# Prompt attention scores as three half-height products per head, two heads side by side, in place of two full-height products

## The chip, the cores and the metric

The kernel runs on one core of a Trainium2 chip. The metric is the device time of one execution in microseconds; the median of the runs of the kernel before is 925.88 us (three runs, 924.18 to 926.4).

## What is computed

One step of a streaming encoder layer: 512 prompt rows and 32 sample rows of 1024 features, all in float32. A projection gives queries, keys, values and gates for two attention mixers. Mixer A has 16 query heads on 4 key heads and a window of three chunks; mixer B has 16 heads with keys of their own and reaches over all earlier chunks. Both end in a gated sum, an output projection and a convolutional feed-forward part. Cut to what matters here:

```python
def attend(q, k, v, bias, sink):
    s = jnp.einsum('bqngd,bknd->bngqk', q, k, preferred_element_type=jnp.float32) * (HEAD_DIM ** -0.5) + bias
    if sink is not None:
        col = jnp.broadcast_to(sink.astype(jnp.float32)[:, :, None, None], s.shape[:-1] + (1,))
        p = jax.nn.softmax(jnp.concatenate([s, col], axis=-1), axis=-1)[..., :-1]
    else:
        p = jax.nn.softmax(s, axis=-1)
    return jnp.einsum('bngqk,bknd->bqngd', p.astype(v.dtype), v)
```

The head dimension is 64, half of the 128 rows of TensorE.

## The kernel before

All activations lie feature by row and token by column. Every float32 operand of a product is kept as two parts, a high part h in the type float32r and the rest l = x - h, so that a product of x and w is h·w_h + l·w_h + h·w_l (`triple`, line 220). TensorE (PE) does nearly all of the work in such triples: the projections run weight tile by weight tile over the 544 columns in two halves of 272 (`dense`, line 232), eight row blocks of 128 each.

Attention is laid between these triples. `Stream` (line 69) keeps a modelled clock of PE; after every triple `step` may run a piece of attention whose modelled latency is over, or start the next head when its queries, keys and values are due and the pace `PACE_A` or `PACE_B` has run out. The resulting program is then put in order for each engine by a scheduler with a timeline of its own, so neighbours in the text need not be neighbours in PE's queue.

Each pair of heads has 128 feature rows, head 0 in rows 0 to 63 and head 1 in rows 64 to 127. Before the scores, `load_q` (line 439) makes one stack of 128 rows for each head: the high part in the head's own 64 rows (ScalarE, line 445) and the low part in the other 64 (VectorE, line 446). The keys are doubled to match: `kh` has the high part twice, above and below, and `kl` the low part twice. The own half is written by `split` (lines 430 and 431), the other half by a DMA from SBUF to SBUF (`dup`, line 434). So a tile of 128 queries needs two products of full height (line 499): stack times `kh` gives qh·kh + ql·kh, and stack times `kl` adds qh·kl + ql·kl. In mixer B every one of the 8 pairs has keys of its own (`pair_b`, line 765, four key tiles and four such DMAs a pair); in mixer A four query heads share a key head (`group_a`, line 691, and `load_ka`, line 639).

`attend_prompt` (line 528) does one head: four tiles of queries, each with two products into a PSUM bank of the pool `psa` (five banks) and a VectorE instruction that adds the bias and takes the row maximum (line 501). In mixer A each tile has 256 key columns; in mixer B the four tiles have 256, 256, 384 and 512. Then come the softmax (ScalarE line 485, GpSimd line 493), the transposes of the probabilities, their split into `pt_h` and `pt_l`, the products with `v` and `fold`. The sample rows have their own small products; those of `pts` with `v_s` (lines 741 and 855) fill only 64 of PE's columns, for the two heads of a pair in the two halves of the columns.

```python
        for t, (pc, k0, n, bc) in enumerate(geo):
            qs = q[:, 128 * t:128 * t + 128]
            scores(p[:, pc:pc + n], [qs, qs], [x[:, k0:k0 + max(n, 256)] for x in (kh, kl)], bias[:, bc:bc + n],
                   floor, mx[:, t:t + 1])
```

Of the kernel before, what the change touches and what calls it, by code (L numbers as in the profile page):

```python
# [8 lines left out]
F32 = mybir.dt.float32  # L9
F32R = mybir.dt.float32r  # L10
# [5 lines left out]
NP = 512  # L16
# [42 lines left out]
PACE_A, PACE_B, PACE_S = 7.09, 5.87, 1.44  # L59
# [9 lines left out]
class Stream:  # L69
# [74 lines left out]
def body(ctx, tc, a, o):  # L144
# [349 lines left out]

    def scores(out, lhs, rhs, bias, floor, mx):
# [4 lines left out]
        ps = ps[:, :out.shape[1]]  # L500
        V.tensor_tensor_reduce(out=out, in0=ps, in1=bias, op0=ALU.add, op1=ALU.max, scale=1.0,  # L501
                               scalar=floor, accum_out=mx)
# [19 lines left out]
    def fetch(name, i, cols, src):  # L522
        t = ap.tile([128, cols], F32, name=name)
        v = t[:, :src.shape[1]]
        load(v, src, "bias")
        return v

    def attend_prompt(q, kh, kl, bias, floor, sinkcol, geo, groups, vt, hh, dst, dh, scored, done):


        p = ap.tile([128, 1280], F32, name="p")
        mx = ap.tile([128, 4], F32, name="mx", bufs=4)
        tiles = []
        for t, (pc, k0, n, bc) in enumerate(geo):
            qs = q[:, 128 * t:128 * t + 128]
            scores(p[:, pc:pc + n], [qs, qs], [x[:, k0:k0 + max(n, 256)] for x in (kh, kl)], bias[:, bc:bc + n],
                   floor, mx[:, t:t + 1])
            tiles.append(slice(pc, pc + n))
        scored()
        with tc.high_priority(LATER):  # L540
            softmax(p, tiles, mx, sinkcol)
        yield LAT_SOFT
        pts = []
        for blocks, n, _ in groups:
            pts.append(transposed(p, blocks, n))
        yield LAT_PT
        po = bank(psa)
        started = False
        last = groups[-1][2][-1]
        for (h, l), (_, _, prods) in zip(pts, groups):  # L550
            for pr in prods:
                j, c, oc, w = pr
                for x in (h, l):
                    mm(po[:, oc:oc + w], lhsT=vt[:, j, hh, :, :], rhs=x[:, c:c + w],
                       start=not started, stop=pr is last and x is l, skip_group_check=True)
                    started = True
        fold(po, dst[:, :NP], dh, NP)
        done()
# [132 lines left out]
    def group_a(j, ka, va):  # L691
# [11 lines left out]
        kuse = Join(4, lambda _: pe.release("k", 2))  # L703
        vuse = Join(4, lambda _: pe.release("v", 1))

        def scored():
            pe.release("q", 1)
            kuse.one()
# [8 lines left out]
        for u in range(2):  # L717
            pe.reserve("q", 2, 5)
            st2 = [ap.tile([128, NP], F32R, name="q", bufs=5) for _ in range(2)]
            ready = []  # L720
            qready.append(ready)

            def sample(zn, u=u):
                for hh, own, other in pair_rows():
                    h = 2 * u + hh
                    nc.scalar.copy(qsam[own, h], zn[own])
                    V.tensor_tensor(qsam[other, h], zn[own], rr(qsam)[own, h], ALU.subtract)
            for hh in range(2):
                h = 4 * j + 2 * u + hh

                def start(bias, u=u, hh=hh, st2=st2, h=h):
                    sc = col("sink", h)
                    return attend_prompt(st2[hh], kh, kl, bias, sc, sc, a_geo, a_groups, vt, half,
                                         oa[u], hh, scored, finished)
                pe.queue(lambda h=h: fetch("bias", h, 512, a["alibi"][h]), start, (ready, ka[2], va[2]), PACE_A)
            dense(head_norm(0, load_q(st2, sample, ready)))

        def pv(po, pt):
            for hh, own, _ in pair_rows():
                for b in range(2):  # L740
# [5 lines left out]
        pe.queue(lambda: fetch("bias_s", j, 288, a["alibi_s"][j]),  # L746
                 lambda bias: attend_sample([q, q], [ka[3][half], ka[4][half]], bias, sc, sc, 2, A_BLK, pv,
# [17 lines left out]
    def pair_b(i, ob, one):  # L765
# [3 lines left out]
        st2 = [ap.tile([128, NP], F32R, name="q", bufs=5) for _ in range(2)]  # L769
# [6 lines left out]
        dense(head_norm(1, load_q(st2, sample, qr)))  # L776
# [10 lines left out]
        def write(s, c0, cn, zn):  # L787
            n = min(cn, NP - c0)
            if s == 0:
                split(ks_hi[:, NS:], ks_lo[:, NS:], raw, G)  # L790
            for hh, own, _ in pair_rows():
                split(kh[hh][own, c0:c0 + n], kl[hh][own, c0:c0 + n], zn[own, :n])
            nc.sync.dma_start(out=o["kb"][i, :, c0:c0 + cn], in_=zn)
            if s == 1:
                split(ks_hi[:, :NS], ks_lo[:, :NS], zn[:, NP - c0:])
                for hh, own, other in pair_rows():
                    dup(kh[hh], own, other)
                    dup(kl[hh], own, other)
                kr.append(pe.clock + LAT_NORM + LAT_DMA)
# [7 lines left out]
        def scored():  # L807
            pe.release("q", 1)
            pe.release("k", 2)
# [4 lines left out]
        for hh in range(2):  # L814
# [7 lines left out]
    def group_b(g):  # L822
# [35 lines left out]
        for u in range(2):  # L858
# [3 lines left out]
        pe.queue(lambda: fetch("bias_s", g, 288, a["rel_s"][g]),  # L862
                 lambda bias: attend_sample(lhs, rhs, bias, -3.0e38, None, 3, B_BLK, pv,
                                            obs, scored_s, finished_s),
                 pairs[1][3], PACE_S, 2)
# [366 lines left out]
```

## Time and profile before

| | |
|---|---|
| median of the runs | 925.88 us |
| the profiled execution, its own time | 924.88 us |
| span of the profiled execution | 923.0 us |
| PE busy | 898.6 us (97%) |
| VectorE (DVE) busy | 723.6 us (78%) |
| ScalarE (ACT) busy | 542.2 us (59%) |
| GpSimd (POOL) busy | 379.1 us (41%) |
| mean granted clock of PE | 0.994 |
| score products of the prompt (line 85, `ps<-k,q`) | 256, from 54.0 to 468 us |

The profile shows one execution. A PE product is listed from its start to a modelled end, so neighbours overlap; what a product costs is read from the distance between starts. "PEld" is the load of a product's stationary operand, which can run ahead of the product. A row of a timeline that ends in xN merges N like instructions: its start is that of the first, its length reaches to the end of the last.

### The profile page before, as it was taken

Reading aid. Unit: us, or ns where it says so; the run is one execution under the profiler, and the core shown is the slowest. Engines: PE = TensorE matmul, PEld = TensorE weight load, DVE = VectorE, ACT = ScalarE, POOL = GpSimd, SP = SyncE. Lnnn points to the kernel's source line nnn. Section 1 sums busy time; section 2 is a strip of 40 time slices with the busy share of each in tenths; the row PEclk is TensorE's granted clock in tenths of the full one; section 3 lists DMA queues with packets and bytes.
Section 4 is the critical chain, followed back from the end, with each engine's and each line's share of the span. In section 5 each row is a group of like instructions: output and inputs, shape, how many; then the busy total and the mean of one; then the engine's idle time right before and its main releaser. Section 6 shows DMA issues by size and latency. Waiting matters only on the chain.

```text
span 923.0 us, 18908 instructions
## 1 busy us (share of the span) xinstructions
PE 898.6 (97%) x7085; PEld 884.4 (96%) x7085; DVE 723.6 (78%) x1471; ACT 542.2 (59%) x1285; POOL 379.1 (41%) x578
## 2 busy tenths in 40 slices
PE   8879999999999999999999999999999999999998
PEld 7879899989989999999999999999999999999998
DVE  7799876868888888998866558768777776886996
ACT  5568777778878777777764244344444443534542
POOL 6534457465876777766541103221222221100100
PEclk9999999999999999999999999999999999999999
DMA  6222222322334443434415222222222222332342
GB/s 216 83 82 88 71 90 85 101 81 75 109 118 122 135 124 109 129 110 136 133 59 168 89 92 92 92 77 85 92 93 92 84 87 83 96 101 81 119 145 67
DMA packets 40012, 94.38 MB, mean 102 GB/s; under 512 B 4944, under 2 KB 16240, under 8 KB 39920
## 3 DMA queue, kind: packets, MB, share of 16 engines
q1 hardware_dynamic: 39920, 93.17, 31.8%
q8 instruction: 56, 0.92, 0.4%
q14 instruction: 36, 0.29, 0.1%
HBM read 80.48 MB, written 7.10 MB: 95 GB/s over the span
## 4 chain that ended last, share of the span: by engine, by line
PE 76%; DVE 9%; ACT 4%; POOL 3%; issue 2%; DMA 0%; DVEq 0%; POOLq 0%
PE ps L85 73%; PE ps L89 3%; ACT p L485 2%; DVE q L446 1%; DVE zn L422 1%; DVE p L501 1%; DVE w_lo L204 1%; POOL p L493 1%; DVE s L254 1%; DVE t_b L319 1%; DVE k L431 1%; POOL t_sql L414 1%; POOL z L421 1%; DVE pt_l L512 0%; DMA k<-k 0%
## 5 line engine op out<-in xcount | busy, mean ns | idle before, releaser
L85 PE MATMUL ps<-xh,w_lo 128*128 128x272 f32 x1536 | 446.3, 292 | 5.1 <-DVE w_lo L204 5.1
L85 PE MATMUL ps<-xh,w_hi 128*128 128x272 f32 x1536 | 446.0, 292 | 2.7 <-ACT z L412 1.7
L85 PE MATMUL ps<-xl,w_hi 128*128 128x272 f32 x1536 | 446.3, 291 | 0.8 <-DVE xl L327 0.8
L85 PEld LDWEIGHTS ps<-xh,w_lo 128*128 128x128 f32 x1536 | 291.6, 190 | 6.5 <-DVE w_lo L204 6.0
L85 PEld LDWEIGHTS ps<-xh,w_hi 128*128 128x128 f32 x1536 | 291.5, 190 | 4.8 <-ACT z L412 1.9
L85 PEld LDWEIGHTS ps<-xl,w_hi 128*128 128x128 f32 x1536 | 292.0, 190 | 2.1 <-DVE xl L327 1.7
L204 DVE TENSOR_TENSOR w_lo<-w_raw,w_hi 128x1024 fp32r<-128x1024 f32 (+2 forms) x112 | 143.2, 1279 | 30.8 <-ACT w_hi L203 18.3
L201 POOL TENSOR_SCALAR w_hi<-w_raw 128x1024 fp32r<-128x1024 f32 (+2 forms) x62 | 66.6, 1075 | 90.2 <-PE ps L85 70.3
L493 POOL TENSOR_SCALAR p<-p,rc 128x256 f32<-128x256 f32 (+3 forms) x128 | 74.2, 596 | 41.4 <-DVE rc L491 38.0
L203 ACT CAST w_hi<-w_raw 128x1024 fp32r<-128x1024 f32 x50 | 52.6, 1051 | 64.9 <-issue 36.1
L85 PE MATMUL ps<-s,w_hi 128*128 128x272 f32 x448 | 84.0, 288 | 0.0
L485 ACT ACTIVATE p<-p,nm 128x256 f32<-128x256 f32 (+3 forms) x128 | 65.4, 514 | 27.8 <-DVE nm L482 27.7
L938 POOL TENSOR_SCALAR state_u<-u 128x2 f32<-128x2 f32 x44 | 17.1, 388 | 148.7 <-DVE u L935 148.7
L85 PE MATMUL ps<-s 128*128 128x272 f32 (+1 forms) x483 | 71.3, 293 | 1.7 <-DVE s L372 1.7
L85 PEld LDWEIGHTS ps<-s,w_hi 128*128 128x128 f32 x448 | 70.1, 188 | 0.0
L935 DVE TENSOR_TENSOR u<-ps,rstd 128x272 f32<-128x272 f32 x88 | 38.5, 441 | 39.6 <-PE ps L85 37.0
L85 PEld LDWEIGHTS ps<-s 128*128 128x128 f32 x483 | 65.1, 190 | 2.2 <-DVE s L372 1.7
L85 PE MATMUL ps<-s,w_lo 128*128 128x272 f32 x224 | 63.8, 288 | 0.0
L85 PE MATMUL ps<-k,q 128*128 128x256 f32 (+2 forms) x256 | 52.1, 308 | 3.5 <-DMA k<-k 1.8
L414 POOL TENSOR_TENSOR t_sql<-t_sq,t_sqh 128x272 fp32r<-128x272 f32 x52 | 52.7, 1014 | 3.7
L421 POOL TENSOR_TENSOR z<-z,t_y 128x272 f32<-128x272 f32 x52 | 42.7, 822 | 23.9 <-ACT t_y L316 21.7
L512 DVE TENSOR_TENSOR pt_l<-ps,pt_h 128x512 fp32r<-128x512 f32 (+1 forms) x80 | 45.6, 602 | 5.5 <-ACT pt_h L511 4.4
(166 smaller groups left out, 1635.1 us busy)
## 6 DMA issues: line engine op xcount, KB each, us to landing
w_raw<-in_w_in SPq DMA_DIRECT2D x50, 512.0 KB, 3.4
w_raw<-in_w_up SPq DMA_DIRECT2D x44, 512.0 KB, 3.3
w_raw<-in_w_pair SPq DMA_DIRECT2D x16, 512.0 KB, 3.4
k<-k SPq DMA_DIRECT2D x40, 128.0 KB, 2.3
bias<-in_rel SPq DMA_DIRECT2D x16, 256.0 KB, 2.7
w_raw<-in_w_out SPq DMA_DIRECT2D x8, 512.0 KB, 3.5
s<-in_x SPq DMA_DIRECT2D x15, 272.0 KB, 5.7
w_raw<-in_w_down SPq DMA_DIRECT2D x6, 512.0 KB, 3.3
```

The costliest lines, as they stand in the source:

```text
L85: return self.nc.tensor.matmul(out, lhsT=lhsT, rhs=rhs, **kw)
L89: return self.nc.tensor.transpose(out, src, ident)
L201: G.tensor_scalar(hi[:, c], raw[:, c], 1.0, 1.0, ALU.mult, ALU.mult)
L203: nc.scalar.copy(hi[:, c], raw[:, c])
L204: V.tensor_tensor(lo[:, c], raw[:, c], rr(hi)[:, c], ALU.subtract)
L414: G.tensor_tensor(sql, sq, rr(sqh), ALU.subtract)
L421: G.tensor_tensor(z, z, y, ALU.mult)
L485: act(p[:, sl], p[:, sl], AF.Exp, bias=nm[:, t:t + 1], accum_out=sm[:, t:t + 1])
L493: G.tensor_scalar(p[:, sl], p[:, sl], rc[:, t:t + 1], 1.0, ALU.mult, ALU.mult)
L512: V.tensor_tensor(l[:, :n], ps[:, :n], rr(h)[:, :n], ALU.subtract)
L935: V.tensor_tensor(u[:, 2 + c0:2 + c0 + cn], ps, rstd2[:, c0:c0 + cn], ALU.mult)
L938: G.tensor_scalar(state_u[:, m, 0:2], u[:, NP:NP + 2], 1.0, 1.0, ALU.mult, ALU.mult)
```

## The change

Two heads are scored at once. `load_q` keeps the pair's queries as they lie, in one tile of high parts and one of low parts; there are no stacks. For each tile of queries two banks are taken, and each head gets three products of 64 rows: qh·kh, qh·kl and ql·kh (the product ql·kl is left out). Head 0's products use rows 0 to 63 of PE, head 1's rows 64 to 127, and the program text alternates between the two. In mixer B the keys need not be doubled: the 32 DMAs of `dup` go, and a pair has two key tiles in place of four. Mixer A's keys stay doubled, since a key head meets queries of both halves. The softmax and the value part stay one per head (`values`, with a later start for the second head), the bias of two heads is fetched into one tile, and the modelled clock counts a product of 64 rows as half.

```diff
-PACE_A, PACE_B, PACE_S = 7.09, 5.87, 1.44
+LAT_TWO = 4.5
+PACE_A, PACE_B, PACE_S = 12.6, 10.2, 1.44
...
-        self.clock += max(n / 2350, 0.108)
+
+        self.clock += max(n / 2350, 0.108) * (0.5 if lhsT.shape[0] == 64 else 1)
...
-    def load_q(stacks, sample, ready):
-
+    def load_q(qh, ql, sample, ready):
         def write(s, c0, cn, zn):
             n = min(cn, NP - c0)
-            for hh, own, other in pair_rows():
-                q = stacks[hh]
-                nc.scalar.copy(q[own, c0:c0 + n], zn[own, :n])
-                V.tensor_tensor(q[other, c0:c0 + n], zn[own, :n], rr(q)[own, c0:c0 + n], ALU.subtract)
+            split(qh[:, c0:c0 + n], ql[:, c0:c0 + n], zn[:, :n])
...
+        ps = [ap.tile([128, 1280], F32, name="p", bufs=4) for _ in range(2)]
+        mx = [ap.tile([128, 4], F32, name="mx", bufs=6) for _ in range(2)]
         tiles = []
         for t, (pc, k0, n, bc) in enumerate(geo):
-            qs = q[:, 128 * t:128 * t + 128]
-            scores(p[:, pc:pc + n], [qs, qs], [x[:, k0:k0 + max(n, 256)] for x in (kh, kl)], bias[:, bc:bc + n],
-                   floor, mx[:, t:t + 1])
+            banks = [bank(psa) for _ in range(2)]
+            w = max(n, 256)
+            for i, (x, y) in enumerate(((0, 0), (0, 1), (1, 0))):
+                for hh, own, _ in pair_rows():
+                    mm(banks[hh][:, :w], lhsT=q[x][own, 128 * t:128 * t + 128], rhs=ks[hh][y][own, k0:k0 + w],
+                       start=i == 0, stop=i == 2)
+            for hh in range(2):
+                biased(ps[hh][:, pc:pc + n], banks[hh], bias[:, hh, bc:bc + n], floor[hh], mx[hh][:, t:t + 1])
             tiles.append(slice(pc, pc + n))
         scored()
-        with tc.high_priority(LATER):
-            softmax(p, tiles, mx, sinkcol)
-        yield LAT_SOFT
+        for hh in range(2):
+            with tc.high_priority(LATER):
+                softmax(ps[hh], tiles, mx[hh], sinkcol and sinkcol[hh])
+            pe.run(values(ps[hh], groups, vt, vh[hh], dst, hh, done))
+        return
+        yield
+
+    def values(p, groups, vt, vh, dst, hh, done):
+        yield LAT_SOFT + LAT_TWO * hh
...
-        pe.reserve("k", 4, 8)
+        pe.reserve("k", 2, 8)
         pe.reserve("ks", 1, 2)
-        kh = [ap.tile([128, NP], F32R, name="k", bufs=8) for _ in range(2)]
-        kl = [ap.tile([128, NP], F32R, name="k", bufs=8) for _ in range(2)]
+        kh, kl = (ap.tile([128, NP], F32R, name="k", bufs=8) for _ in range(2))
...
-            for hh, own, _ in pair_rows():
-                split(kh[hh][own, c0:c0 + n], kl[hh][own, c0:c0 + n], zn[own, :n])
+            split(kh[:, c0:c0 + n], kl[:, c0:c0 + n], zn[:, :n])
             nc.sync.dma_start(out=o["kb"][i, :, c0:c0 + cn], in_=zn)
             if s == 1:
                 split(ks_hi[:, :NS], ks_lo[:, :NS], zn[:, NP - c0:])
-                for hh, own, other in pair_rows():
-                    dup(kh[hh], own, other)
-                    dup(kl[hh], own, other)
-                kr.append(pe.clock + LAT_NORM + LAT_DMA)
+                kr.append(pe.clock + LAT_NORM)
...
-        for hh in range(2):
-            def start(bias, hh=hh):
-                return attend_prompt(st2[hh], kh[hh], kl[hh], bias, -3.0e38, None, b_geo, b_groups, vt, hh,
-                                     ob, hh, scored, finished)
-            pe.queue(lambda hh=hh: fetch("bias", i, 512, a["rel"][2 * i + hh]), start, (qr, kr, vr), PACE_B)
+
+        def start(bias):
+            return attend_prompt(qn, [(kh, kl)] * 2, bias, [-3.0e38] * 2, None, b_geo, b_groups, vt, (0, 1),
+                                 ob, scored, finished)
+        pe.queue(lambda: fetch("bias", 512, a["rel"][2 * i], a["rel"][2 * i + 1]), start, (qr, kr, vr), PACE_B)
```

PE's queue at the first scores of mixer A, before. A row is a product: the bank it writes, then the moving and the stationary operand, then the size of the result. `ps_744` to `ps_756` are the banks of head 0's four query tiles, `q_230` its stack, `k_207` and `k_209` the doubled keys, and `ps_788` belongs to a projection:

```order
L85 MATMUL ps_788<-xh0_109,w_lo_457 128x272
L85 MATMUL ps_744<-k_207,q_230 128x256
L85 MATMUL ps_744<-k_209,q_230 128x256
L85 MATMUL ps_748<-k_207,q_230 128x256
L85 MATMUL ps_748<-k_209,q_230 128x256
L85 MATMUL ps_788<-xh1_123,w_hi_456 128x272
```

The same place in the changed program, and, fifteen projection products further on, the rest of the second tile and part of the third. `q_230` and `q_231` are the pair's high and low queries; `ps_740` and `ps_741` are the banks of head 0 and of head 1 for the first tile, `ps_750` that of head 0 for the second, `ps_751` that of head 1 for the second, and `ps_760` that of head 0 for the third:

```order
L87 MATMUL ps_720<-xh6_160,w_hi_458 128x272
L87 MATMUL ps_740<-k_207,q_230 128x256
L87 MATMUL ps_741<-k_207,q_230 128x256
L87 MATMUL ps_740<-k_209,q_230 128x256
L87 MATMUL ps_741<-k_209,q_230 128x256
L87 MATMUL ps_750<-k_207,q_230 128x256
L87 MATMUL ps_750<-k_209,q_230 128x256
L87 MATMUL ps_720<-xl6_161,w_hi_458 128x272
L87 MATMUL ps_720<-xh6_160,w_lo_459 128x272
L87 MATMUL ps_740<-k_207,q_231 128x256
L87 MATMUL ps_741<-k_207,q_231 128x256
L87 MATMUL ps_750<-k_207,q_231 128x256
```

```order
L87 MATMUL ps_824<-xh3_142,w_lo_459 128x272
L87 MATMUL ps_751<-k_207,q_230 128x256
L87 MATMUL ps_751<-k_209,q_230 128x256
L87 MATMUL ps_751<-k_207,q_231 128x256
L87 MATMUL ps_824<-xh4_150,w_hi_458 128x272
L87 MATMUL ps_760<-k_207,q_230 128x256
L87 MATMUL ps_760<-k_209,q_230 128x256
L87 MATMUL ps_760<-k_207,q_231 128x256
L87 MATMUL ps_824<-xl4_151,w_hi_458 128x272
```

The text's alternation stands in the first tile; from the second on the scheduler has put the three products of one head together, and products of a projection between the heads. Over the whole queue the 384 products of 64 rows stand in 77 unbroken runs (48 of three products, 17 of six, 5 of nine, 4 of twelve, 3 of fifteen); 47 of the runs hold one head alone. Of the 307 neighbours within runs 118 are of different heads.

VectorE's queue where the first pair's queries are written, before and after (`zn` is the normed pair, 272 and 240 columns of it):

```order
L446 TENSOR_TENSOR q_230<-zn_563,q_230 64x272
L446 TENSOR_TENSOR q_231<-zn_563,q_231 64x272
L204 TENSOR_TENSOR w_lo_643<-w_raw_641,w_hi_642 128x1024
L446 TENSOR_TENSOR q_230<-zn_582,q_230 64x240
L446 TENSOR_TENSOR q_231<-zn_582,q_231 64x240
```

```order
L321 SCALAR_TENSOR_TENSOR t_b_579<-ps_573,eps_80,t_b_579 128x272
L463 TENSOR_TENSOR v_217<-ps_626,v_217 128x8x64
L424 SCALAR_TENSOR_TENSOR zn_582<-t_b_579,z_443 128x272
L292 TENSOR_TENSOR s_636<-ps_687,rstd_179 128x272
L433 TENSOR_TENSOR q_231<-zn_565,q_230 128x272
L433 TENSOR_TENSOR q_231<-zn_582,q_230 128x240
```

Two instructions on all 128 rows stand where four on 64 rows stood; ScalarE's copies halve in the same way, and so do those of mixer B's keys.

## Rows read from the trace of the kernel before

**Rows 1.** The page: busy time, share of the span and instructions of each engine.
```profile
PE 898.6 (97%) x7085; PEld 884.4 (96%) x7085; DVE 723.6 (78%) x1471; ACT 542.2 (59%) x1285; POOL 379.1 (41%) x578
```

**Rows 2.** The page: the chain that ended last, share of the span by engine.
```profile
PE 76%; DVE 9%; ACT 4%; POOL 3%; issue 2%; DMA 0%; DVEq 0%; POOLq 0%
```

**Rows 3.** Busy us of each engine in the stretch of the scores.
```profile
core 0: us, PE busy (x) PEld busy (x) DVE busy (x) ACT busy (x) POOL busy (x), PEclk, DMA share, GB/s
54.00:468.00 414.00, 400.62 (x3175) 390.60 (x3174) 344.70 (x800) 317.27 (x891) 256.40 (x335) 0.99 0.34 104
```

**Rows 4.** Timeline: the eight score products of mixer B's last head, the product behind.
```profile
466.54 1.45 PE L85 MATMUL ps<-k,q 128*128 128x256 f32 x8
...
467.83 0.29 PE L85 MATMUL ps<-xh,w_hi 128*128 128x272 f32 x1
```

**Rows 5.** Timeline: 64-column products, then four scores of mixer A, then a triple.
```profile
114.64 0.46 PE L85 MATMUL ps<-pts,v_s 80*64 80x64 f32 x8
...
115.03 0.53 PEld L85 LDWEIGHTS ps<-k,q 128*128 128x128 f32 x4
115.03 0.74 PE L85 MATMUL ps<-k,q 128*128 128x256 f32 x4
...
115.60 0.29 PE L85 MATMUL ps<-xh,w_lo 128*128 128x272 f32 x1
```

**Rows 6.** Timeline: triples, eight 64-column products, full-width products again.
```profile
152.41 0.29 PE L85 MATMUL ps<-xh,w_hi 128*128 128x272 f32 x1
...
152.53 0.29 PE L85 MATMUL ps<-xl,w_hi 128*128 128x272 f32 x1
152.74 0.32 PEld L85 LDWEIGHTS ps<-pts,v_s 80*64 80x64 f32 x8
152.75 0.46 PE L85 MATMUL ps<-pts,v_s 80*64 80x64 f32 x8
...
153.13 0.19 PEld L85 LDWEIGHTS ps<-t_sqh,bdiag 128*128 128x128 f32 x1
153.13 0.39 PE L85 MATMUL ps<-t_sqh,bdiag 128*128 128x272 f32 x1
...
153.36 0.29 PE L85 MATMUL ps<-t_sql,bdiag 128*128 128x272 f32 x1
```

**Rows 7.** Groups by form, whole span: the 64-column products and their loads.
```profile
L85 PE MATMUL ps<-pts,v_s 80*64 80x64 f32 x32 | 1.8, 234 | 0.0
...
L85 PEld LDWEIGHTS ps<-pts,v_s 80*64 80x64 f32 x32 | 1.3, 136 | 0.5
```

**Rows 8.** Timeline: loads of full width behind products of 128 columns.
```profile
151.81 0.19 PEld L85 LDWEIGHTS ps<-pt_l,v 128*128 128x128 f32 x1
...
151.92 0.19 PEld L85 LDWEIGHTS ps<-xh,w_hi 128*128 128x128 f32 x1
```

**Rows 9.** Timeline: a transpose with 32 columns between triples.
```profile
285.46 0.29 PE L85 MATMUL ps<-xl,w_hi 128*128 128x272 f32 x1
...
285.47 0.10 PEld L89 LDWEIGHTS ps<-ident,s 128*32 128x32 f32 x1
285.59 0.27 PE L89 MATMUL ps<-ident,s 128*32 128x128 f32 x1
```

**Rows 10.** PE's waits from 54 to 468 us: us in total, times, longest.
```profile
PE ps L85 <- DVE w_lo L204: 2.9, 1, 2.9
PE ps L89 <- DVE t_b L319: 1.9, 1, 1.9
PE ps L85 <- DMA k<-k: 1.8, 1, 1.8
```

**Rows 11.** Groups on DVE, 54 to 468 us: low parts of queries and keys.
```profile
L446 DVE TENSOR_TENSOR q<-zn,q 64x272 fp32r<-64x272 f32 x31 | 18.2, 588 | 2.5 <-ACT q L445 1.5
L446 DVE TENSOR_TENSOR q<-zn,q 64x240 fp32r<-64x240 f32 x32 | 15.5, 485 | 2.1 <-ACT q L445 1.2
L431 DVE TENSOR_TENSOR k<-zn,k 64x272 fp32r<-64x272 f32 x18 | 11.2, 624 | 3.7 <-ACT k L430 3.4
L431 DVE TENSOR_TENSOR k<-zn,k 64x240 fp32r<-64x240 f32 x18 | 9.7, 537 | 2.2 <-ACT k L430 1.8
```

**Rows 12.** Windows with a lower clock (columns as in rows 3).
```profile
68.00:76.00 8.00, 6.92 (x43) 6.92 (x44) 8.00 (x21) 7.37 (x21) 0.00 (x0) 0.79 0.31 92
...
100.00:120.00 20.00, 18.14 (x139) 17.52 (x138) 16.31 (x35) 14.74 (x37) 10.49 (x14) 0.91 0.09 27
```

More of the change, by code (lines that the diff above doesn't have):

```diff
@@ L493, in softmax, with biased @@
             G.tensor_scalar(p[:, sl], p[:, sl], rc[:, t:t + 1], 1.0, ALU.mult, ALU.mult)
+    def biased(out, ps, bias, floor, mx):
+        V.tensor_tensor_reduce(out=out, in0=ps[:, :out.shape[1]], in1=bias, op0=ALU.add, op1=ALU.max, scale=1.0,
+                               scalar=floor, accum_out=mx)
     def scores(out, lhs, rhs, bias, floor, mx):
@@ L499, in scores @@
             mm(ps[:, :rhs[i].shape[1]], lhsT=lhs[i], rhs=rhs[i], start=i == 0, stop=i == n - 1)
-        ps = ps[:, :out.shape[1]]
-        V.tensor_tensor_reduce(out=out, in0=ps, in1=bias, op0=ALU.add, op1=ALU.max, scale=1.0,
-                               scalar=floor, accum_out=mx)
+        biased(out, ps, bias, floor, mx)
     def transposed(p, blocks, n):
@@ L520, in fold, with fetch, attend_prompt @@
         V.tensor_tensor(dst[own], po[own], t[own, :n], ALU.add)
[L522 to L525, printed above, removed]
[L526 to L532 removed]
+    def fetch(name, cols, *srcs):
+        t = ap.tile([128, len(srcs), cols], F32, name=name)
+        v = t[:, :, :srcs[0].shape[1]]
+        for i, src in enumerate(srcs):
+            load(v[:, i], src, "bias")
+        return v
+    def attend_prompt(q, ks, bias, floor, sinkcol, geo, groups, vt, vh, dst, scored, done):
+        ps = [ap.tile([128, 1280], F32, name="p", bufs=4) for _ in range(2)]
+        mx = [ap.tile([128, 4], F32, name="mx", bufs=6) for _ in range(2)]
         tiles = []
         for t, (pc, k0, n, bc) in enumerate(geo):
[L535 to L537 removed]
+            banks = [bank(psa) for _ in range(2)]
[6 more added lines that the diff above has]
+                biased(ps[hh][:, pc:pc + n], banks[hh], bias[:, hh, bc:bc + n], floor[hh], mx[hh][:, t:t + 1])
             tiles.append(slice(pc, pc + n))
         scored()
[L540 to L542 removed]
+        for hh in range(2):
[6 more added lines that the diff above has]
+        yield LAT_SOFT + LAT_TWO * hh
         pts = []
@@ L718, in group_a @@
             pe.reserve("q", 2, 5)
-            st2 = [ap.tile([128, NP], F32R, name="q", bufs=5) for _ in range(2)]
+            qn = [ap.tile([128, NP], F32R, name="q", bufs=5) for _ in range(2)]
             ready = []
@@ L727, in sample, with start @@
                     V.tensor_tensor(qsam[other, h], zn[own], rr(qsam)[own, h], ALU.subtract)
-            for hh in range(2):
[L729 to L736, printed above, removed]
+            hs = [4 * j + 2 * u + hh for hh in range(2)]
+            def start(bias, u=u, qn=qn, hs=hs):
+                sc = [col("sink", h) for h in hs]
+                return attend_prompt(qn, [(kh, kl)] * 2, bias, sc, sc, a_geo, a_groups, vt, (half, half),
+                                     oa[u], scored, finished)
+            pe.queue(lambda hs=hs: fetch("bias", 512, *(a["alibi"][h] for h in hs)), start,
+                     (ready, ka[2], va[2]), PACE_A)
+            dense(head_norm(0, load_q(*qn, sample, ready)))
         def pv(po, pt):
@@ L745, in group_a @@
         sc = col("sink_s", j)
-        pe.queue(lambda: fetch("bias_s", j, 288, a["alibi_s"][j]),
-                 lambda bias: attend_sample([q, q], [ka[3][half], ka[4][half]], bias, sc, sc, 2, A_BLK, pv,
+        pe.queue(lambda: fetch("bias_s", 288, a["alibi_s"][j]),
+                 lambda bias: attend_sample([q, q], [ka[3][half], ka[4][half]], bias[:, 0], sc, sc, 2, A_BLK, pv,
                                             oa, lambda: pe.release("ks", 1), finished_s),
@@ L768, in pair_b @@
         pe.reserve("q", 2, 5)
-        st2 = [ap.tile([128, NP], F32R, name="q", bufs=5) for _ in range(2)]
+        qn = [ap.tile([128, NP], F32R, name="q", bufs=5) for _ in range(2)]
         qr, kr, vr = [], [], []
@@ L861, in group_b @@
             rhs += [pairs[u][1], pairs[u][2], pairs[u][1]]
-        pe.queue(lambda: fetch("bias_s", g, 288, a["rel_s"][g]),
-                 lambda bias: attend_sample(lhs, rhs, bias, -3.0e38, None, 3, B_BLK, pv,
+        pe.queue(lambda: fetch("bias_s", 288, a["rel_s"][g]),
+                 lambda bias: attend_sample(lhs, rhs, bias[:, 0], -3.0e38, None, 3, B_BLK, pv,
                                             obs, scored_s, finished_s),
-                 pairs[1][3], PACE_S, 2)
+                 pairs[1][3], PACE_S, 1)
     for g in range(4):
```

13 lines of the change are left out of this document (6 added, 7 removed).

## The prediction

> **What bounds the kernel now.** I read the page first. PE is busy for 97% of the span, DVE for 78% [rows 1], and PE holds 76% of the chain that ended last [rows 2]; so the reader should count in PE's time. Then I cut out the stretch in which the scores stand, 54 to 468 us: PE is busy 400.6 of 414.0 us there, DVE 344.7, ACT 317.3 [rows 3]. PE has 13.4 us of gaps in this stretch and everything else on it is queue behind queue. What lengthens PE's queue lengthens the kernel; what unburdens the others is worth at most those gaps.
>
> **What a score product costs now.** In the timeline the reader is to see starts, since the listed lengths overlap. Mixer B's last head issues its eight products (four of 256 columns, two of 384, two of 512) at 466.54 and the next product starts at 467.83: 1.29 us a head [rows 4]. In units of 256 columns that head is 4 + 3 + 4 = 11, so one unit takes 0.117 us. Mixer A agrees: four products of 256 columns and the start of the one behind them take 115.03 to 115.60, 0.57 us [rows 5], of which about 0.11 is a first load of weights that had nothing to hide behind (full-width loads follow each other 0.11 us apart [rows 8]). So mixer A's heads cost 8 x 0.117 = 0.94 us each, and all scores 16 x 1.29 + 16 x 0.94 = 35.6 us of PE.
>
> **Part 1, three products in place of two.** In single file the change costs PE 35.6 x 1.5 = 53.4 us. If each product of head 0 ran fully beside one of head 1 it would be half of that, 26.7. What stands between is the order in PE's queue. The program text alternates, the queue does so only in part: of 307 neighbours in unbroken runs, 118 are of different heads, and 47 of the 77 runs hold one head alone. I let a product start with its predecessor if it is of the other half and that half is free, and otherwise when its half is free. Walked through all 77 runs with slots of 0.117, 0.174 and 0.232 us (256, 384, 512 columns), this saves 9.9 us: 54 of the 256-column products, 22 of 384 and 11 of 512 start beside another, some for part of their length only. So 53.4 - 9.9 = 43.5 us, **7.9 us more** than now. Bounds: -8.9 with every pair side by side, +17.8 with none.
>
> No product of this trace uses half of the rows. The nearest are the `pts` products, which use half of the columns, two heads alternating. Eight of their loads take 0.32 us from the first start to the last end, and one is listed with 136 ns [rows 6, 7]: the last starts 0.18 us after the first. A load of 64 columns should need half of the 0.11 us of a full one, 0.055, and seven in single file 0.39. So the two halves do go side by side, and I take that for the halves of the rows too.
>
> **Part 2, going into half mode and back.** Rows 6 show something else. Full products start 0.12 us apart (152.41, 152.53). The first `pts` load comes only at 152.74, 0.21 us after the last full product started, although loads otherwise run ahead of it. The eight products end at 153.21 as listed; with 0.23 us for one [rows 7] the last starts at about 152.98, and the next full load comes 0.15 us later, at 153.13. Its product is again held back by its own load: the one behind it starts 0.23 us later in place of 0.125. From 152.53 to 153.36 are 0.83 us. Two full products need 0.25 and eight `pts` in pairs 4 x 0.055 = 0.22. The remaining **0.36 us is lost at the two borders**: PE empties itself before it goes from whole to half, and again on the way back. In the timeline of 114.64 the way out looks the same, with 115.03 for the next load [rows 5]. A score product has 128 stationary columns, so its first load behind the border takes 0.11 in place of 0.055 us: I take 0.41 us for one run. 77 runs x 0.41 = **31.6 us**. Bounds: nothing, as at the transposes with 32 columns, whose load starts 0.01 us after the product before and whose product comes 0.13 us after it [rows 9]; and 0.5 us, 38.5 in all, if a 512-column product holds a border longer. I take the `pts` price, because these rows too pair two halves of the array, and the transpose has no partner half. The products before the change stand in runs too, but of full height, and paid no border.
>
> The Trainium skill has a rule that speaks against this change: "TensorEngine Tiling (Array Packing)", Key Properties, says that a change of tiling mode, and not merely of tile, drains TensorE. By that rule the rows of `pts` are the pattern for every run and the sum keeps its 31.6 us; by the same page's Theoretical Speedup (up to twice for 64 rows), taken alone, the term would be nothing and part 1 would be -8.9. Rows 6 agree with the first for halves of the columns; no run here shows it for halves of the rows.
>
> **Part 3, what the other engines save.** In this stretch DVE writes 63 low parts of queries of 0.54 us on the mean (33.7 us in all) and 36 of keys [rows 11]. The queries' instructions halve and so do those of mixer B's keys (32 to 16, 0.58 us each): 17 + 9 = 26 us less for DVE, as many instructions less for ACT, and 32 transfers with their place in SP's queue. All of it lies beside PE, so it pays only through PE's 13.4 us of gaps. The longest are waits for the low part of a weight, for a norm and for one doubled key (2.9, 1.9, 1.8 us) [rows 10]; two drag a lower clock behind them, 0.79 over 8 us and 0.91 over 20 [rows 12], 0.21 x 8 + 0.09 x 20 = 3.5 us in which PE stood at 1.2 in place of 2.4 GHz, counted at full speed. With PE later by a tenth and DVE lighter, others are on time more often, but new waits come: eight banks are asked for almost at once by two heads where `psa` has five, and DVE must empty each; behind a score product that waits for a bank stand the projection's triples, and behind those all the rest. I take half of the gaps, **-6.8 us**; bounds 0 and -16.9 (all gaps and the clock). The doubled bias fetch moves the same bytes. The values of the second head start 4.5 us later on the modelled clock, and the last pair's end then stands inside the output projection, with 50 of its products still ahead of the first that needs the last gated sum, 50 x 0.125 = 6 us: I cost that at nothing; if that cover failed, it would be a wait of a few us.
>
> **Sum.** 924.9 (profiled execution) + 7.9 + 31.6 - 6.8 = 957.6. The profiled execution lies 1.0 us under the median of the runs shown, so I say **958 us**. A difference of 0.3%, 2.8 us, is about what a measurement of this kernel tells from none.
>
> **Rivals.**
> *No overlap of the row halves, but the borders.* Against it speaks the overlap of the column halves. 924.9 + 17.8 + 31.6 - 6.8 = 967.5; with 0.5 us a border more.
> *No border for halves of the rows, and no overlap.* 924.9 + 17.8 - 6.8 = 936.
> *No border, overlap as in the queue.* The transposes speak for it, `pts` against it. 924.9 + 7.9 - 6.8 = 926, no change.
> *Faster.* The borders cost nothing and the gaps, not the products, decide: without 26 us of DVE work and the doubling DMAs, PE's waits go altogether, and the falls of the clock with them. 924.9 + 7.9 - 16.9 = 916. This needs a border under (16.9 - 7.9) / 77 = 0.12 us. For it: DVE is busy 83% of the stretch [rows 3]. Against it: the measured border is three times that. That every pair ran side by side, as the text asks (924.9 - 8.9 - 6.8 = 909), is kept out by the queue's order; it has 0.03 of this case. "Up to twice" from the page named above would give that 909.
>
> **How the numbers follow.** My forecast 0.60, no overlap with borders 0.13, no overlap without 0.08, overlap without borders 0.10, faster 0.09. Slower takes the first three and 0.03 of the fourth: 0.84; no change 0.07; faster 0.09. The range reaches down into the case of 926, to 925, and up past 967.5, to 970; what is left out is the faster case, the lower half of the 926 case and a few hundredths above. The forecast's own range, with 0.3 to 0.5 us a border and 0 to -13 of relief, is 943 to 971.
>
> **What would show it.** Right: at each run of `k,q` with 64 rows the first load starts about 0.21 us after the last full product, and the next full load 0.2 us after the last half product; two products of different heads start within some 0.02 us of each other; 256-column products of one head 0.117 apart; PE's gaps from 54 on below 13 us; DVE's busy time about 26 us lower. Wrong: loads of 64 rows that run ahead of full products with no hole (then 926 or less), or halves that wait for each other (then 967).

## The result, and the profile after

The changed kernel takes **967.51 us** (median of four runs, 966.93 to 969.24) where the kernel before takes 926.14 beside it: 1.0453 times as long, 95% interval 1.0431 to 1.0474. The forecast was 958 us, with a range to 970. The profiled execution takes 969.24 us, 44.4 more than the profiled one of before.

The page of the changed kernel: the line of busy times, the chain that ended last, and the score products as a group:

```profile
PE 939.1 (97%) x7213; PEld 897.1 (93%) x7213; DVE 690.5 (71%) x1423; ACT 520.4 (54%) x1237; POOL 371.7 (38%) x578
...
PE 45%; DVE 0%; issue 0%
...
L87 PE MATMUL ps<-k,q 64*128 64x256 f32 (+2 forms) x384 | 60.5, 328 | 0.4 <-DVE t_b L321 0.4
```

Beside [rows 1] DVE has lost 33 us and ACT 22, and PE has gained 40: the other engines were unburdened as meant, and the kernel got longer with PE. The chain goes back only to 520.6 us, behind the last scores, and says nothing of them. The 384 products of 64 rows stand in the trace from 55 to 512 us. That stretch, with the columns of [rows 3]:

```profile
54.00:512.00 458.00, 442.29 (x3317) 406.72 (x3316) 311.60 (x748) 296.37 (x835) 253.23 (x336) 0.98 0.27 85
```

PE has 15.7 us of gaps in it, in place of the 13.4 of [rows 3] (13.4 before in these same 458 us, too); they were to shrink. Now one border. The timeline from 56.78 us shows a projection product, a run of six score products of both heads, and the projection again:

```profile
56.78 0.29 PE L87 MATMUL ps<-xh,w_lo 128*128 128x272 f32 x1
...
56.99 0.42 PEld L87 LDWEIGHTS ps<-k,q 64*128 64x128 f32 x6 [0.15 <-issue]
57.00 0.63 PE L87 MATMUL ps<-k,q 64*128 64x256 f32 x6
...
57.55 0.19 PEld L87 LDWEIGHTS ps<-xh,w_hi 128*128 128x128 f32 x1
57.56 0.40 PE L87 MATMUL ps<-xh,w_hi 128*128 128x272 f32 x1
```

The first load of 64 rows starts 0.21 us after the last full product, as the first `pts` load did in [rows 6]. The six products come as three pairs, 0.35 us from the first start to the last: first starts at 56.997 and 57.007 us, the next pair 0.22 us later behind its own load, the third 0.12 after that. The next full load starts 0.2 us after the last of them, and the product behind `xh,w_hi` 0.23 us after it. Over all 77 runs the median way in is 0.217 us, the way out 0.206 us behind 256 columns (0.26 behind 384, 0.32 behind 512), the next start 0.231. What that adds to undisturbed distances, with the 0.107 us by which the second load of a run shows, is 32.1 us in all, **0.416 us a run**.

What PE waited for in the changed kernel (total us, times, longest), the whole span:

```profile
PE ps L87 <- ACT z L414: 4.7, 3, 3.7
PE ps L87 <- DVE pt_l L512: 4.3, 4, 2.0
PE ps L87 <- ACT pt_h L511: 3.2, 2, 2.1
```

These take the place of the waits of [rows 10]: neither a doubled key nor the norm `t_b` stands first now, but ACT and the split of the probabilities.

**A ledger for all runs.** I sum the distances between the starts of neighbouring PE products. A projection product is taken out at its undisturbed distance (0.125 us for 272 columns, 0.117 for 256, 0.109 for 128, other widths in proportion); what is left of the intervals that touch a run of score products, the one behind the first full product included, is "scores and borders", what is left of all others is "lost elsewhere" (over the whole span). Before: 41.2 and 37.1. After: 70.8 and 51.5. So of the 44 us, 29.6 lie at the scores and 14.4 are new loss in places without any score product.

### The profile page after: what moved, and what is told of

Same layout as the page of the kernel before. It is cut to its first block, busy times and chain, and to the rows that moved or that the text cites. A ratio compares the mean times of both kernels' runs of the same rounds, so it can differ in the third digit from the quotient of the medians.

```text
span 967.5 us, 18977 instructions
## 1 busy us (share of the span) xinstructions
PE 939.1 (97%) x7213; PEld 897.1 (93%) x7213; DVE 690.5 (71%) x1423; ACT 520.4 (54%) x1237; POOL 371.7 (38%) x578
## 5 line engine op out<-in xcount | busy, mean ns | idle before, releaser
L206 DVE TENSOR_TENSOR w_lo<-w_raw,w_hi 128x1024 fp32r<-128x1024 f32 (+2 forms) x112 | 146.3, 1307 | 48.0 <-POOL w_hi L203 29.4
L415 POOL TENSOR_SCALAR t_sqh<-t_sq 128x272 fp32r<-128x272 f32 x52 | 26.4, 508 | 90.7 <-PE ps L87 71.0
L87 PE MATMUL ps<-k,q 64*128 64x256 f32 (+2 forms) x384 | 60.5, 328 | 0.4 <-DVE t_b L321 0.4
L511 ACT CAST pt_h<-ps 128x512 fp32r<-128x512 f32 (+1 forms) x80 | 38.9, 526 | 31.1 <-PE ps L91 23.3
```

What stands on the lines that cost most here:

```text
L206: V.tensor_tensor(lo[:, c], raw[:, c], rr(hi)[:, c], ALU.subtract)
L415: G.tensor_scalar(sqh, sq, 1.0, 1.0, ALU.mult, ALU.mult)
L511: nc.scalar.copy(h[:, :n], ps[:, :n])
```

## The experiments

All times are medians of four runs with the kernel before beside them (923.8 to 925.4 us); the ratio's 95% interval is in brackets. The order in which they are told is by question.

**1. The border: the same program on all rows.**

```diff
-                    mm(banks[hh][:, :w], lhsT=q[x][own, 128 * t:128 * t + 128], rhs=ks[hh][y][own, k0:k0 + w],
-                       start=i == 0, stop=i == 2)
+                    mm(banks[hh][:, :w], lhsT=q[x][:, 128 * t:128 * t + 128], rhs=ks[hh][y][:, k0:k0 + w],
+                       half=True, start=i == 0, stop=i == 2)
```

> The changed kernel with the same instructions in the same order, but every score product takes all 128 rows of queries and keys, so nothing is ever in half mode and nothing can run side by side (each head's scores then hold the other head's product too; the rest is untouched). Theory (borders): in the changed kernel's trace the 77 runs lose 32.1 us at their borders and their products take 40.1 us; here no border, 53.2 us of products: 967.5 - 32.1 + 13.1 = 948 us, and loads ahead of every score product. Rival (the borders only fill time in which PE would have waited anyway, and the third product is what costs): 967.5 + 13.1 = 980 us.

Measured: 951.32 us, 1.0294 [1.027, 1.0318], 16.2 less than the changed kernel although its products can't run beside each other. The same instructions in the same order; the timeline has no hole at a run:

```profile
57.17 0.28 PE L87 MATMUL ps<-xh,w_lo 128*128 128x272 f32 x1
57.29 0.54 PE L87 MATMUL ps<-k,q 128*128 128x256 f32 x3
...
57.66 0.29 PE L87 MATMUL ps<-xh,w_hi 128*128 128x272 f32 x1
```

In at 0.12 us, three products in 0.37. The ledger gives 55.4 us at the scores (70.8 after) and 50.0 elsewhere (51.5 after). Without borders the kernel is 16.2 us shorter although its score products take 53.2 us in place of 40.1: 29.3 us for 77 runs, 0.38 a run. So the border is shown and is near the size forecast, and the loss elsewhere has nothing to do with half mode: it is there without a single border.

**2. The border with one head at a time.** Here `scores` is called for one head after the other with three products, at the pace of before; first on all rows (told under 4, 934.85 us), then on the head's own 64 rows with the order unchanged.

```diff
+        own = pair_rows()[hh][1]
...
-            scores(p[:, pc:pc + n], [q[x][:, 128 * t:128 * t + 128] for x in (0, 0, 1)],
-                   [ks[y][:, k0:k0 + w] for y in (0, 1, 0)], bias[:, bc:bc + n], floor, mx[:, t:t + 1])
+            scores(p[:, pc:pc + n], [q[x][own, 128 * t:128 * t + 128] for x in (0, 0, 1)],
+                   [ks[y][own, k0:k0 + w] for y in (0, 1, 0)], bias[:, bc:bc + n], floor, mx[:, t:t + 1])
```

> The order of the run with one head at a time and all 128 rows (934.9 us), instruction for instruction, but each score product on the 64 rows of its own head, so that the scores are the reference's again. 83 runs of score products, none of them with two heads in it. Theory (0.41 us per run, whatever the handling of heads): 934.9 + 83 x 0.41 = 969 us, since nothing runs beside anything; score products and borders cost some 34 us more of TensorE than in that run. Rival (TensorE has waits there that the borders merely fill): 945 to 955 us.

Measured: 959.13 us, 1.0389 [1.0364, 1.0415]. Both missed. The scores rose by 26.9 us in the ledger (64.0 to 90.9) and not by 34: on all rows the runs already held 10.8 us of first loads and waits beside their 53.2 us of products. Elsewhere the ledger fell by 7.5 us (28.7 to 21.2), but 3.7 of these lie before 54 us, where the profiled run on all rows was granted 0.91 of the clock and the other 1.00. PE's gaps in the stretch of the scores, with all rows and then with half of them:

```profile
54.00:512.00 458.00, 449.69 (x3570) 440.47 (x3570) 338.89 (x786) 317.07 (x884) 264.01 (x348) 0.99 0.29 94
```

```profile
54.00:512.00 458.00, 454.02 (x3396) 421.74 (x3397) 322.41 (x762) 304.21 (x858) 256.08 (x345) 0.99 0.26 86
```

8.3 us of gaps become 4.0. That the others catch up while PE stands at a border fits this, but no run shows it by itself. By the medians, 24.3 us for 83 runs are 0.29 us of time for a border that costs 0.41 beside undisturbed distances.

**3. Which products run beside each other.** Three runs tried to bring the text's alternation into PE's queue, to shorten the products and, in one of them, the number of runs. The first two put the products of one tile, or of two, into a unit that the scheduler must not split.

```diff
+            with tc.tile_critical():
+                for i, (x, y) in enumerate(((0, 0), (0, 1), (1, 0))):
+                    for hh, own, _ in pair_rows():
+                        mm(banks[hh][:, :w], lhsT=q[x][own, 128 * t:128 * t + 128], rhs=ks[hh][y][own, k0:k0 + w],
+                           start=i == 0, stop=i == 2)
```

> The changed kernel with the six half-height products of one query tile kept together as one unit, strictly alternating between the heads: 61 runs in place of 77, every product beside one of the other head. Theory (borders and overlap add up on PE): products 26.6 us in place of 40.1, borders 61 x 0.416 = 25.4 in place of 32.1: 967.5 - 20 = 947 us, a few us more if PE now waits until both banks are free. Rival (halves do not gain from the order, or the waits of the other engines set the time): 963 to 970 us.

> As unit_tile, but twelve products of two query tiles are one unit: 29 runs, all in pairs, four PSUM banks asked for at once. Theory: products 26.6 us, borders 29 x 0.416 = 12.1 us: 967.5 - 13.5 - 20.0 = 934 us, plus whatever PE waits for four banks. Rival (waits for banks grow as the runs grow fewer and give it back): 947 us or more, not under unit_tile.

Measured: 1059.76 us, 1.1458 [1.1425, 1.1492], and 1033.48 us, 1.1172 [1.1137, 1.1207]. Both missed by far; the unit itself spoilt them. The timeline of the run with units of two tiles:

```profile
207.34 0.29 PE L87 MATMUL ps<-xl,w_hi 128*128 128x272 f32 x1
207.47 0.29 PE L87 MATMUL ps<-xh,w_lo 128*128 128x272 f32 x1
208.24 0.98 PE L87 MATMUL ps<-k,q 64*128 64x256 f32 x12 [0.48 <-ACT q_sa L744]
```

A unit is entered 0.77 us after the last product here, not 0.21; in the run with units of one tile the median is 1.03. In PE's queue a wait for semaphores and a branch of 0.18 us stand at this entry, at 207.89 and 208.00 us. 61 entries at 0.81 us above the usual make 50 of the 92 us by which units of one tile are longer than the change. The twelve products themselves do overlap, 0.70 us from first to last start, six pairs of 0.117. About fewer borders these two say nothing. The third run chains each product to the one before it instead.

```diff
+            last = None
...
+                for hh, own, _ in reversed(pair_rows()):
+                    with tc.issue_after(last.ins) if last else nullcontext():
+                        last = mm(banks[hh][:, :w], lhsT=q[x][own, 128 * t:128 * t + 128],
+                                  rhs=ks[hh][y][own, k0:k0 + w], start=i == 0, stop=i == 2)
```

> The changed kernel with the six products of a tile chained in the order of writing, so that the heads really alternate: 73 runs instead of 77, 21 of them of a single product, most others of five or more. Theory (0.41 us per run, products of the two halves beside each other): 4 borders fewer give 1.6 us, products walked with full overlap take 30 us instead of the 40 that the changed kernel's trace shows, so 955 to 958 us. Rival (the overlap is complete already, in whatever order the products stand, and only borders count): 964 to 967 us, or more where the chained order makes new waits.

Measured: 978.07 us, 1.0585 [1.0548, 1.0621]: missed on the slow side. The products did what was expected, 31.3 us in the trace against 40.1, and the ledger's scores fell from 70.8 to 63.8; but elsewhere it lost 66.2 in place of 51.5, most of it at one wait:

```profile
PE ps L91 <- POOL p L491: 16.0, 9, 3.1
```

Nine times PE stands before the transposes of probabilities that POOL has not finished. Why the chain makes them late was not followed up. So the question of order was asked again with the heads in blocks:

```diff
-            for i, (x, y) in enumerate(((0, 0), (0, 1), (1, 0))):
-                for hh, own, _ in reversed(pair_rows()):
+            for hh, own, _ in reversed(pair_rows()):
+                for i, (x, y) in enumerate(((0, 0), (0, 1), (1, 0))):
```

> The changed kernel with the six products of a tile chained head by head, three of one and then three of the other: 76 runs, 32 of them with products of both heads, those in blocks of three. Theory (the two halves run beside each other in whatever order the products stand in the queue, and a run lasts as long as the longer half's products): the products take 39.5 us in the trace. Rival (a product starts only behind all that stand ahead of it in the queue, as the forecast walked it): 46 us. A run of three and three of 256 columns, first start to last start: 0.35 us by the theory, 0.58 us by the rival. The whole: 966 to 982 us, since chaining brought about 15 us of waits where the heads alternated.

Measured: 966.64 us, 1.0465 [1.0444, 1.0486], and 40.2 us for the products. Of the run's timeline, six products that stand in the program's queue as three of one head and three of the other (the profile does not name the heads):

```profile
302.09 0.30 PE L87 MATMUL ps<-ks_hi,qs_lo 128*128 128x288 f32 x1
302.32 0.63 PE L87 MATMUL ps<-k,q 64*128 64x256 f32 x6
302.87 0.39 PE L87 MATMUL ps<-xh,w_hi 128*128 128x272 f32 x1
```

The full product behind starts 0.55 us after the first, of which 0.2 is the way out: 0.35 us for six, the same as where the heads alternate. In single file the last of six would start 0.11 + 5 x 0.117 = 0.69 us after the first, and by the rule of the forecast 0.58. The theory holds: a run lasts as long as the products of its longer half, whatever the order. Only the distance within a pair tells the orders apart: 0.003 us in the median where the program alternates (the chained run and the units of two tiles), 0.010 here.

**4. The loss elsewhere: is it the pairing of heads?** One head at a time, three products on all rows, no stacks, pace of before:

```diff
-PACE_A, PACE_B, PACE_S = 12.6, 10.2, 1.44
+PACE_A, PACE_B, PACE_S = 7.09, 5.87, 1.44
...
+            scores(p[:, pc:pc + n], [q[x][:, 128 * t:128 * t + 128] for x in (0, 0, 1)],
+                   [ks[y][:, k0:k0 + w] for y in (0, 1, 0)], bias[:, bc:bc + n], floor, mx[:, t:t + 1])
...
+        yield from values(p, groups, vt, vh, dst, hh, done)
```

> The changed kernel with every score product on all 128 rows (both heads' scores are added up, so the prompt scores are not the reference's) and one head at a time again, with the pace of the kernel before; three products per tile, no stacks, no doubled keys. Theory (the pair handling made the new waits): score products and borders cost 55 us of TensorE as in the same run with pairs, the other intervals lie near their 37 us of before instead of 50, so 951.3 - 13 = 938 us, less if the lighter VectorE gives something back. Rival (the waits come from another part of the change: new splits of queries and keys, or three products on a tile instead of two): 951 us, other intervals still near 50.

Measured: 934.85 us, 1.0111 [1.0078, 1.0144], 16.5 less than the same products in pairs. The theory's side, by more than it asked. (Its profiled execution, 939.2 us, is the longest of its four, so its ledger, 64.0 and 28.7, is some 4 us too high in sum.) Against before, the third product costs 53.2 - 35.6 = 17.6 us of PE and the kernel got only 9 to 11 longer: here the lighter engines did give back some 7 to 8 us. Whether DVE, ACT or the transfers that went gave them is not separated.

And the other way round: the stacks, the doubled keys and the two full products of before, but two heads at a time as in the change.

```diff
+            for hh in range(2):
+                for i in range(2):
+                    mm(banks[hh][:, :w], lhsT=q[hh][:, 128 * t:128 * t + 128], rhs=ks[hh][i][:, k0:k0 + w],
+                       start=i == 0, stop=i == 1)
```

> The changed kernel with the stacks of queries, the doubled keys with their DMAs and two full-height products per head as in the kernel before, but still two heads at a time with the new paces. PE's score work is that of the kernel before (35.6 us, no border). Theory (the part of the loss that borders and products do not explain, some 12 to 14 us, comes from handling two heads at once, two softmaxes in a row on ScalarE): 936 to 942 us. Rival (it comes from the borders, which put the other engines out of step): 926 us, within 3.

Measured: 968.18 us, 1.0474 [1.045, 1.0499]. Both missed: without half mode, without a third product, the pairing and its paces alone cost the kernel before 44 us, most of it elsewhere (76.6 in place of 37.1). What PE waited for most, and the doubled keys:

```profile
PE ps L91 <- POOL p L495: 12.9, 10, 3.5
...
PE ps L87 <- DMA k<-k: 1.4, 2, 1.1
```

**5. Which part of the pairing.** In the changed kernel's timeline one pair of mixer A looks like this on ACT (the exponentials of line 483, the cast of line 511, the sink term of line 486), on PE and on POOL:

```profile
129.68 0.40 ACT L483 ACTIVATE p<-p,nm 128x128 f32<-128x128 f32 x1 [2.99 <-DVE nm L480]
...
133.40 0.50 ACT L483 ACTIVATE p<-p,nm 128x256 f32<-128x256 f32 x1
...
133.89 0.28 ACT L486 ACTIVATE es<-nm,cols 128x4 f32<-128x4 f32 x1
134.08 0.46 ACT L511 CAST pt_h<-ps 128x384 fp32r<-128x384 f32 x1
```

```profile
131.18 0.38 PE L87 MATMUL ps<-pt_h,v 128*128 128x256 f32 x1 [1.17 <-ACT pt_h L511]
...
134.59 0.58 PE L87 MATMUL ps<-pt_h,v 128*128 128x256 f32 x1 [2.06 <-ACT pt_h L511]
```

```profile
134.75 2.55 POOL L491 TENSOR_SCALAR p<-p,rc 128x128 f32<-128x128 f32 x6 [8.98 <-ACT es L486]
```

The eight exponentials of both heads stand back to back on ACT for 4.2 us; what the previous pair still needs from ACT (`pt_h`) stands among and behind them, and POOL can't divide either head before `es`, behind all eight. The next run moves the second head's softmax alone, its transposes and products with `v` stay where they were:

```diff
         for hh in range(2):
-            with tc.high_priority(LATER):
-                softmax(ps[hh], tiles, mx[hh], sinkcol and sinkcol[hh])
-            pe.run(values(ps[hh], groups, vt, vh[hh], dst, hh, done))
+            pe.run(values(ps[hh], tiles, mx[hh], sinkcol and sinkcol[hh], groups, vt, vh[hh], dst, hh, done))
...
-        yield LAT_SOFT + LAT_TWO * hh
+        if hh:
+            yield LAT_TWO
+        with tc.high_priority(LATER):
+            softmax(p, tiles, mx, sink)
+        yield LAT_SOFT
```

> The changed kernel, with the second head's softmax written into the order 4.5 us of TensorE's clock behind the first head's instead of straight behind it; 80 runs of score products instead of 77. Theory (the burst of eight exponentials on ScalarE is what makes TensorE wait): most of the 14 us of new waits goes, 3 more borders cost 1.2 us, so 955 to 961 us. Rival (the burst is covered, the waits are of another kind): 966 to 970 us.

Measured: 957.63 us, 1.0354 [1.0324, 1.0385], 9.9 less than the change; the ledger's loss elsewhere falls from 51.5 to 36.8. Theory. The same edit in the two other paired programs:

> Every score product on all 128 rows (both heads' scores added up, so the prompt scores are not the reference's), pairs as in the changed kernel, and the second head's softmax 4.5 us later. Theory (burst): 951.3 - 6 to 12 = 939 to 945 us, since there is no border that could hide or add anything. Rival: 949 to 953 us.

Measured: 947.40 us, 1.0239 [1.0216, 1.0262], 3.9 less than without the edit: the right direction, but between the theory (6 to 12 less) and the rival.

> Two heads at a time with stacks, doubled keys and two full-height products (968.2 us), and now the second head's softmax 4.5 us later. Theory (the burst of two softmaxes makes the waits wherever heads go in pairs): at least the 10 us that the same edit gave in the changed kernel, since the waits are larger here (some 39 us more than in the kernel before): 945 to 958 us. Rival (the waits come from the stacks and doubled keys being late when two heads need them at once): 964 to 970 us.

Measured: 962.48 us, 1.0425 [1.0405, 1.0445], 5.7 less. Neither theory: the burst has a part in it, and 69.9 us are still lost elsewhere. With the stacks and doubled keys of two heads something else is late as well. It is not the doubled keys that PE stands for (1.4 us without the edit, none with it); POOL's `p` still stands first, with 7.9 us in place of 12.9. Why `p` is late there stays open. Last, a larger distance:

```diff
-LAT_TWO = 4.5
+LAT_TWO = 7.0
```

> The changed kernel with the second head's softmax 7.0 us of TensorE's clock behind the first's instead of 4.5 us. Theory (what pairing still costs, some 12 us beside the run with one head at a time once the overlap of the halves is counted, is the two softmaxes lying too close): evenly spaced heads take more of it away, 948 to 954 us. Rival (the softmax was done with at 4.5 us; the rest comes from two heads' tiles being written out of the banks in one burst, or from the pace): 955 to 960 us.

Measured: 949.85 us, 1.0295 [1.0266, 1.0324], 17.7 less than the change and inside the theory's range, with 81 runs of score products and so no fewer borders. The loss elsewhere is 31.5 us. ACT's row for the same pair, and the stretch of the scores:

```profile
131.59 0.40 ACT L483 ACTIVATE p<-p,nm 128x128 f32<-128x128 f32 x1 [7.04 <-DVE nm L480]
...
134.08 0.29 ACT L486 ACTIVATE es<-nm,cols 128x4 f32<-128x4 f32 x1
134.27 0.39 ACT L483 ACTIVATE p<-p,nm 128x128 f32<-128x128 f32 x1
134.78 0.58 ACT L511 CAST pt_h<-ps 128x512 fp32r<-128x512 f32 x1
```

```profile
54.00:512.00 458.00, 449.76 (x3473) 416.66 (x3472) 329.73 (x771) 309.73 (x872) 270.26 (x352) 1.00 0.26 87
```

Here `es` of the first head comes 2.5 us after its first exponential (4.2 in the change), and the cast gets in between the second head's. PE's gaps are 8.2 us, half of the change's 15.7, and the clock is full. The larger distance also moves the second head's values by 2.5 us, so the 7.8 us beyond the run before it are not the softmaxes' alone. This is the fastest version with half-height products, and it is still 26 us behind the kernel before; no run beats that one.

## Why the prediction was right, and where it was not

**The side and the size: right.** Slower, by 41 us at the medians where 32 were forecast, inside the range. That the size came out so near is luck: two steps erred in opposite directions.

**Going into half mode and back: right.** 31.6 us were forecast, 77 runs of 0.41; the trace has 32.1, 0.416 each. The price taken from the `pts` rows, halves of the columns, holds for halves of the rows, and the lower bound, the transposes that pay nothing, was rightly put aside. The rule of the Trainium skill that was weighed there ("TensorEngine Tiling (Array Packing)", Key Properties: a change of mode drains) agrees with this trace for halves of the rows too: 0.21 us each way. Both rivals without a border fall, and with them no change and faster. But a border beside undisturbed distances is not a border in time: 0.38 us a run in experiment 1 and 0.29 in experiment 2, where the runs on all rows had loads and waits of their own.

**Three products in place of two: a term too large.** 43.5 us were forecast, 40.1 measured. The step that failed is the walk: "I let a product start with its predecessor if it is of the other half and that half is free". The halves do not keep to the queue's order; by the longer half of each run the walk gives 39.2 us. The rival without overlap, 967.5 us, met the measured time to the digit and is wrong all the same: in single file the products would take 53.2 us.

In the ledger products and borders together cost 29.6 us more than before, where 7.9 + 31.6 = 39.5 were forecast. 3.4 of the difference is that walk; most of the rest is on the other side, for the runs of before cost 41.2 in the ledger and not 35.6: first loads and short waits at their 94 runs had been left out.

**What the other engines save: wrong in sign.** Relief of 6.8 us was forecast, 14.4 us of loss came. The engines were lighter as counted (DVE by 33 us, 26 forecast), and with one head at a time the relief is there, some 7 to 8 us (experiment 4). The step that failed is what the pairing costs. I named the banks as the place of new waits; most of it was two softmaxes, and the values behind them, coming at once (the second softmax alone 9.9 us, with its values 17.7). I costed the second head's later values at the output projection alone, and did not ask what two softmaxes at once do to ACT's and POOL's queues. By medians, from 934.85 us: pairing 16.5, then half rows 16.2 (borders 32, overlap -13, the rest in waits), makes 967.5. Spacing the two heads takes 17.7 back. The paces changed with the pairing and were not tried alone; the run that takes 17.7 back keeps them.

The clock follows the waits. ACT's `z` and the product that waits for it, then two windows of the changed kernel, at a pair of mixer B, and the stretch around the same time in the last version:

```profile
451.19 0.47 ACT L414 ACTIVATE z<-ps,gains 128x272 f32<-128x272 f32 x1
...
451.71 0.59 PE L87 MATMUL ps<-xh,w_hi 128*128 128x272 f32 x1 [3.65 <-ACT z L414]
```

```profile
450.00:452.00 2.00, 0.29 (x1) 0.29 (x2) 0.18 (x1) 2.00 (x7) 1.90 (x5) 0.87 0.03 9
452.00:458.00 6.00, 6.00 (x54) 5.81 (x54) 3.88 (x8) 3.45 (x13) 3.78 (x6) 0.76 0.08 25
```

```profile
440.00:470.00 30.00, 30.00 (x228) 27.92 (x226) 21.27 (x50) 19.44 (x57) 17.13 (x23) 1.00 0.21 72
```

After a wait of 3.65 us for ACT's `z`, which stands behind eight exponentials, PE is granted 0.76 for 6 us, so part of them at 1.2 in place of 2.4 GHz; in the last version PE has no wait between 440 and 470 us, and no such stretch.

## What to carry to other kernels

Count how often the queue goes from full products to products on halves of the array and back before counting the rows that stand empty: at 0.41 us a round trip, a run of them must save more than that, which three products of one head (no overlap) or six of 256 columns in pairs (0.35 us) can't. When work is grouped for one engine, follow the group through the other queues: what was spread out by a pace arrives there as a burst, and behind it stands work of the group before. And a program that errs on two terms of opposite sign can meet a time; only the terms, measured one by one, show it.

## What the runs showed of the hardware

Products in the two halves of the rows run beside each other even where three of one half stand in the queue ahead of three of the other: six of 256 columns take 0.35 us from first to last start either way, starts of a pair 0.003 to 0.01 us apart. The Trainium skill ("TensorE: Matmul & The Clock Gate", Part 3) says that products keep strictly to program order; the times of these runs do not agree with that for products of different row halves. Going from full products to products of 64 rows and back cost 0.416 us a run here, and next to nothing where the same products took all rows (55.4 us in the ledger for 53.2 us of products, experiment 1).
